# Two layer seams, the first transfers and the rings of the second mixer's queries in a two-layer fp32 encoder

## The chip, the cores and the metric

The kernel runs on one core of a Trainium2 chip. The metric is the device time of one execution in microseconds; of several runs the median counts. PE is TensorE (matmuls), DVE is VectorE, ACT is ScalarE, POOL is GpSimd; SP only issues DMAs. Each engine works through its own list of instructions in order and waits on semaphores for the others.

## The reference, cut to what matters

The input `x` is (1, 1024, 1024): 1024 tokens of width 1024; `mem` holds 256 memory tokens. There are two layers. Each normalises `x`, projects it once, runs a token mixer and beside it four cross-attention heads into the memory, brings both through one output projection, normalises that, adds the residual, and ends with a gated feed-forward block (ConvGLU, width 2816, depthwise convolution of width 3 along the tokens).

- Layer 0's mixer is a windowed grouped-query attention with rotary positions and sinks.
- Layer 1's mixer (HGRN2) has 8 heads of width 128. It is a gated linear recurrence over the tokens, forwards and backwards: a query q with a SiLU, two forget gates f and b, a value v, an output gate gs; each head's output is normalised over its 128 values and multiplied by a gain.

All of it is float32.

## The kernel before

**Products.** An fp32 operand is held as a high part (rounded, `...h`) and a low part (the rest, `...l`); a product of two such operands is three matmuls (`mm3`). A weight piece of 128 x 1024 floats (512 KB) is loaded into one of four staging buffers (`st`, pool `stage`), cast by ACT to its high part (`wh`), and DVE subtracts to get the low part (`wl`); `wunit` does this, into a ring of four. The staging buffer is free when DVE has subtracted.

**Order of the work.** A tile framework turns the program into one list per engine, by program order, priorities (`tc.high_priority(AHEAD)`) and placement hints (`tc.issue_after(x)`: not ahead of x), and sets the semaphores. A tile from a pool with `bufs=n` waits until the readers of the tile it replaces are done. So every edit can shift the order elsewhere.

**Stages in order.** (1) The start: memory tokens `mT`, the gains `gT` and the first weights are loaded (`start`, L1335 on); ACT makes `mh = mT * gT`, and PE computes the memory's keys and values of both layers, stored to DRAM (`kvd`). (2) The projections and attention of layer 0, to about 420 us. (3) Its output projection and feed-forward block. (4) The second mixer (`hgrn`), about 1235 to 1915 us. Each head projects q, f, b, v, gs (`proj_fm`, `proj_tm`); q is made in two halves of 512 tokens (b = 0, 1), each read by two of the head's four directions, taken in the order (forward, half 0), (backward, half 1), (forward, half 1), (backward, half 0). POOL writes `qin = EP * q` (L1209) as the last reader of q in a direction. `cross_head` loads one memory head's keys and values (`kvh`, `kvl`). `output` normalises the head's result (`on`), PE transposes it (`pt`, L1259), and for the last head ACT and DVE make from it high and low parts of the projection's operand (`uh`, `ul`). (5) The output projection of layer 1 (`Out.finish`): two column halves, 8 token blocks each; for the second half, of each block of 128 tokens: the matmuls into `pb`, sum of squares, `x` = residual plus normalised result, stored to `h1d`, then `norm_T`: `nu` = normalised `x`, 8 PE transposes into `pt`, and a split into `uh`, `ul`. (6) The second feed-forward block (`ffn`): `plain` computes its first unit directly (gi, gj with `wg`, ui, uj with `wu`: `X`, `Y`, `V` banks); the further units use operands that are sums and differences of `uh`/`ul` (`operands`, among them `u7l`) with the weights loaded at L662 and L666.

## Time and profile before

| | |
|---|---|
| three runs | 2661.21, 2664.71, 2666.81 us |
| median | 2664.71 us |
| the profiled execution's own time | 2661.84 us |
| its span, first to last instruction | 2659.7 us |
| PE busy | 2601.1 us (98%) |
| DVE, ACT, POOL busy | 1818.5, 1378.5, 469.6 us |
| DMA | 425.93 MB, 160 GB/s on average |

PE is the engine that is nearly always busy, so what it waits for is what there is to gain or lose. In a row of the timeline stand: start, duration, engine, line, operation, output <- inputs, and in brackets the idle time before it and what ended it. In a row of waits: engine and tile, what it waited for, total us, times, longest. In a row of windows: the stretch, its length, busy time and instructions of PE, of its weight loads, DVE, ACT and POOL, the granted PE clock, the DMA engines' share and GB/s. A queue on SP or ACT (`SPq`) is one on which DMAs are issued.

### The profile page before, as it was taken

Reading aid. Unit: us, or ns where it says so; the run is one execution under the profiler, and the core shown is the slowest. Engines: PE = TensorE matmul, PEld = TensorE weight load, DVE = VectorE, ACT = ScalarE, POOL = GpSimd, SP = SyncE. Lnnn points to the kernel's source line nnn. Section 1 sums busy time; section 2 is a strip of 40 time slices with the busy share of each in tenths; the row PEclk is TensorE's granted clock in tenths of the full one; section 3 lists DMA queues with packets and bytes.
Section 4 is the critical chain, followed back from the end, with each engine's and each line's share of the span. In section 5 each row is a group of like instructions: output and inputs, shape, how many; then the busy total and the mean of one; then the engine's idle time right before and its main releaser. Section 6 shows DMA issues by size and latency. Waiting matters only on the chain.

```text
span 2659.7 us, 39101 instructions
## 1 busy us (share of the span) xinstructions
PE 2601.1 (98%) x14420; PEld 2184.7 (82%) x14420; DVE 1818.5 (68%) x3043; ACT 1378.5 (52%) x2503; POOL 469.6 (18%) x519
## 2 busy tenths in 40 slices
PE   8999999999999999999999999999999999999998
PEld 7888887788888888887888878888888788888887
DVE  6778886578655565478688686887757755656447
ACT  6467676545444445455464554555534444445443
POOL 0321010211111100031224131231211111110013
PEclk9999999999999999999999999999999999999999
DMA  9782232367777857674236351103436778775666
GB/s 354 247 172 57 74 90 82 103 190 193 199 202 193 210 153 257 191 249 150 84 112 153 82 124 52 52 25 103 134 124 178 193 193 209 198 203 166 225 191 237
DMA packets 195728, 425.93 MB, mean 160 GB/s; under 512 B 20048, under 2 KB 56272, under 8 KB 189904
## 3 DMA queue, kind: packets, MB, share of 16 engines
q1 hardware_dynamic: 161840, 325.11, 37.9%
q0 software_dynamic: 24544, 90.19, 16.4%
q10 hardware_dynamic: 9152, 8.14, 1.0%
q8 instruction: 113, 1.85, 0.3%
q14 instruction: 79, 0.65, 0.1%
HBM read 330.04 MB, written 116.39 MB: 168 GB/s over the span
## 4 chain that ended last, share of the span: by engine, by line
PE 82%; DVE 10%; ACT 3%; DMA 3%; issue 1%; POOL 1%; SPq 0%; ACTq 0%; DVEq 0%; POOLq 0%
PE X L557 29%; PE V L557 11%; PE pj L81 6%; PE pj L82 6%; PE pj L83 6%; PE Y L557 5%; PE pb L81 4%; PE pb L83 4%; PE pb L82 4%; DVE E L1146 1%; PE po L1249 1%; PE pt L383 1%; DVE ER L1181 1%; PE pt L116 1%; PE pu L1225 1%
## 5 line engine op out<-in xcount | busy, mean ns | idle before, releaser
L87 DVE TENSOR_TENSOR wl<-st,wh 128x1024 fp32r<-128x1024 f32 (+1 forms) x238 | 262.3, 1109 | 318.8 <-ACT wh L86 280.1
L86 ACT CAST wh<-st 128x1024 fp32r<-128x1024 f32 (+1 forms) x238 | 222.4, 937 | 287.6 <-PE X L557 190.3
L81 PE MATMUL pj<-uh,wh 128*128 128x512 f32 x512 | 202.9, 397 | 4.8 <-DVE q L1091 2.6
L557 PE MATMUL X<-wl,wh 128*128 128x512 f32 x528 | 204.7, 390 | 0.0
L557 PE MATMUL X<-wh,wl 128*128 128x512 f32 x528 | 204.6, 389 | 0.0
L82 PE MATMUL pj<-ul,wh 128*128 128x512 f32 x512 | 201.7, 394 | 0.1
L83 PE MATMUL pj<-uh,wl 128*128 128x512 f32 x512 | 201.7, 394 | 0.0
L557 PE MATMUL X<-wh 128*128 128x512 f32 x528 | 198.7, 390 | 0.9 <-ACT c L963 0.9
L81 PE MATMUL pj<-wh,uh 128*128 128x384 f32 (+1 forms) x512 | 189.7, 371 | 4.7 <-DVE gs L1077 2.5
L83 PE MATMUL pj<-wh,ul 128*128 128x384 f32 (+1 forms) x512 | 187.2, 366 | 0.0
L82 PE MATMUL pj<-wl,uh 128*128 128x384 f32 (+1 forms) x512 | 186.7, 365 | 0.0
L77 DVE TENSOR_TENSOR wl<-st,wh 128x1024 fp32r<-128x1024 f32 (+1 forms) x92 | 116.7, 1275 | 26.4 <-ACT wh L76 25.7
L557 PE MATMUL V<-uh,wh 128*128 128x512 f32 x344 | 133.8, 389 | 0.0
L557 PE MATMUL V<-ul,wh 128*128 128x512 f32 x344 | 133.8, 389 | 0.0
L557 PE MATMUL V<-uh,wl 128*128 128x512 f32 x344 | 133.8, 389 | 0.0
L76 ACT CAST wh<-st 128x1024 fp32r<-128x1024 f32 (+1 forms) x98 | 98.8, 1014 | 47.8 <-PE pj L82 25.4
L557 PEld LDWEIGHTS X<-wh 128*128 128x128 f32 x528 | 99.1, 188 | 21.9 <-ACT c L963 1.3
L81 PEld LDWEIGHTS pj<-uh,wh 128*128 128x128 f32 x512 | 96.3, 188 | 24.9 <-DVE q L1091 3.5
L557 PEld LDWEIGHTS X<-wl,wh 128*128 128x128 f32 x528 | 99.1, 188 | 20.7 <-DVE wl L87 0.3
L557 PEld LDWEIGHTS X<-wh,wl 128*128 128x128 f32 x528 | 99.1, 188 | 20.6
L932 POOL TENSOR_TENSOR c<-c,g 128x512 f32<-128x512 f32 x24 | 43.7, 1838 | 388.5 <-PE X L557 160.1
L83 PEld LDWEIGHTS pj<-uh,wl 128*128 128x128 f32 x512 | 96.2, 188 | 18.7
(399 smaller groups left out, 7212.6 us busy)
## 6 DMA issues: line engine op xcount, KB each, us to landing
st<-hid SPq DMA_DIRECT2D x154, 256.0 KB, 3.0
st<-in_ffw_dram SPq DMA_DIRECT2D x108, 256.0 KB, 3.1
w2s<-in_ffw_dram POOLq DMA_DIRECT2D x24, 1024.0 KB, 9.0
st<-in_ffw_dram SPq DMA_DIRECT2D x46, 512.0 KB, 4.4
hid<-tt SPq DMA_DIRECT2D x88, 256.0 KB, 4.8
st<-w2s SPq DMA_DIRECT2D x88, 256.0 KB, 3.4
sx<-in_ffw_dram SPq DMA_DIRECT2D x84, 256.0 KB, 3.9
sy<-in_ffw_dram SPq DMA_DIRECT2D x42, 512.0 KB, 6.9
```

Source lines behind the costliest of these rows:

```text
L76: act.copy(h[:, :n], raw)
L77: (eng or dve).tensor_tensor(l[:, :n], raw, h[:, :n].bitcast(F32), op=ALU.subtract)
L81: pe.matmul(o, ah, bh, start=first, stop=False)
L82: pe.matmul(o, ah, bl, start=False, stop=False)
L83: pe.matmul(o, al, bh, start=False, stop=last)
L86: act.copy(h, src)
L87: dve.tensor_tensor(l, src, h.bitcast(F32), op=ALU.subtract)
L116: pe.transpose(ps[:, k, :], u[:, (4 * b + k) * P:(4 * b + k + 1) * P], ident)
L383: pe.transpose(tp[:, j, :], sm[:, j, c * P:(c + 1) * P], ident)
L557: last = pe.matmul(o, x, y, start=new, stop=e, skip_group_check=not first)
L932: pool.tensor_tensor(y[q][:, t, :], y[q][:, t, :], g3[:, c], op=ALU.mult)
L1146: dve.tensor_tensor_scan(B[:, rev], smask, a_[:, rev], 0.0, op0=ALU.mult, op1=ALU.add)
```

## The change

- **Start.** The first 128 rows of `mT` are issued first on SP, the next on ACT; the first weight piece comes in three parts of 256, 256 and 512 columns, not in two halves.
- **Second mixer.** q is taken from two rings, one for each half of the tokens: two buffers for half 0 and one for half 1, not one ring of three. The load of keys and values in layer 1 gets priority.
- **Seam 1.** The last transposes of the mixer (last head, half 0) are put behind the matmuls of the projection's third token block; their tiles are moved to the projection's pool, and the gain is copied by POOL. The first weights of the second feed-forward block (`wg`) are loaded early, into tiles that share the space of `qin`.
- **Seam 2.** The last two token blocks keep `nu` in a staging buffer each; their transposes stand behind the 24 matmuls of gi.
- In `operands`, the sum `more` gets the priority that its split has.

```diff
-    def norm_T(pl, pst, src, g, dh, dl, t, tag="n"):
+    def norm_T(pl, pst, src, g, dh, dl, t, tag="n", kept=None):
...
+        u = pl.tile([P, D], F32, tag=tag + "u", name=tag + "u") if kept is None else kept
...
+        def turn():
+            for b in range(2):
...
+        if kept is None:
+            turn()
+        return turn
...
-        nc.sync.dma_start(raw, kvd[l][h])
+        with tc.high_priority(AHEAD) if l else nullcontext():
+            nc.sync.dma_start(raw, kvd[l][h])
...
-                self.cross(ps, t, True, False)
+                crossed = self.cross(ps, t, True, False)
...
+                if l == 1 and i == 2:
+                    with tc.issue_after(crossed.ins):
+                        self.last(psp.tile([P, 4, P], F32, tag="pt", name="pt"))
...
-            self.first = wunit(A["ffw1"][l, 0, :, :1024], pl=self.wf) if l == 0 else None
+            self.first = wunit(A["ffw1"][l, 0, :, :1024], pl=self.wf, tags=(None, ("qin0", "qin1"))[l])
...
-                norm_T(wp, psp, x, g2, uh, ul, t)
-            psp.release()
+                kept = stg.tile([P, D], F32, tag="st", name="nu") if l and t in self.order[6:] else None
+                turn = norm_T(wp, psp, x, g2, uh, ul, t, kept=kept)
+                if kept is not None:
+                    self.turns.append(turn)
...
-            some(wg, gi, range(KT), ti, True)
+            done = some(wg, gi, range(KT), ti, True)
+            for turn in wo.turns:
+                with tc.issue_after(done.ins):
+                    turn()
...
-                more(q, x, B[1], kk, ALU.subtract)
                 with tc.high_priority(AHEAD):
+                    more(q, x, B[1], kk, ALU.subtract)
                     out_of(split, 7, kk, q)
...
+        wo1.wf = tc.alloc_tile_pool(name="hgi", bufs=1, side="right", reuse_waits="tile")
...
-                    q = eq.tile([P, 512], F32, tag="q", bufs=3, name="q")
+                    q = eq.tile([P, 512], F32, tag=f"q{b}", bufs=2 - b, name="q")
...
+            final = h == 7 and b == 0
+            on = (wo1.w1 if final else wp).tile([P, 4, P], F32, tag="on", bufs=1, name="on")
...
+                if final:
+                    pool.tensor_copy(gain, bng[:, h:h + 1])
+                    wo1.last = last
+                else:
+                    last(bank("pt"))
...
-            qin = [wp.tile([P, T], F32, tag=f"qin{d}", bufs=1, name="qin") for d in range(2)]
+            qin = [wo1.wf.tile([P, T], F32, tag=f"qin{d}", bufs=1, name="qin") for d in range(2)]
...
-        for k in (0, 2):
-            act.dma_start(mT[:, k:k + 2], A["memT"][:, k:k + 2])
+        nc.sync.dma_start(mT[:, 0:1], A["memT"][:, 0:1])
+        act.dma_start(mT[:, 1:2], A["memT"][:, 1:2])
+        act.dma_start(mT[:, 2:4], A["memT"][:, 2:4])
...
-        for p in range(2):
-            nc.sync.dma_start(raw0[:, p * 512:(p + 1) * 512], A["wmk"][0, 0, :, p * 512:(p + 1) * 512])
+        for c in (slice(0, 256), slice(256, 512), slice(512, 1024)):
+            nc.sync.dma_start(raw0[:, c], A["wmk"][0, 0, :, c])
```

**Seam 1 on PE.** Before: the last matmuls of the first two token blocks (`pb_18460`, `pb_18487`), the transposes of `on` into `pt`, and the first matmuls of the third block (`pb_18514`).

```order
L83 MATMUL pb_18460<-xwh_18178,ul_78 128x512
L83 MATMUL pb_18487<-xwh_18178,ul_78 128x512
L1259 MATMUL pt_18251<-ident_74,on_18246 128x128 x4
L81 MATMUL pb_18514<-wh_17982,oh_18515 128x512
L82 MATMUL pb_18514<-wl_17983,oh_18515 128x512
L83 MATMUL pb_18514<-wh_17982,ol_18516 128x512
```

After: the third block's last matmuls, the same transposes, and the fourth block (`pb_18548`).

```order
L82 MATMUL pb_18514<-xwl_18184,uh_77 128x512
L83 MATMUL pb_18514<-xwh_18183,ul_78 128x512
L1284 MATMUL pt_18538<-ident_74,on_18251 128x128 x4
L81 MATMUL pb_18548<-wh_17987,oh_18549 128x512
L82 MATMUL pb_18548<-wl_17988,oh_18549 128x512
```

The four transposes moved behind all 18 matmuls of the third block.

**Seam 2 on PE.** Before: the end of the last token block (`pb_19277`), the transposes of the block before it, then gi (`X_19396`).

```order
L83 MATMUL pb_19277<-xwh_18708,ol_19302 128x512
L116 MATMUL pt_19263<-ident_74,nu_19256 128x128 x4
L116 MATMUL pt_19270<-ident_74,nu_19256 128x128 x4
L557 MATMUL X_19396<-uh_77,wh_19384 128x512
L557 MATMUL X_19396<-ul_78,wh_19384 128x512
```

After: the end of gi (`X_19374`, its weights in the space of `qin`), the transposes of both last blocks (`nu_19268`, `nu_19333`), two matmuls of ui (`Y_19375`, weights `wu`), two on the first weight loaded at L686 (`X_19569`), and ui again.

```order
L576 MATMUL X_19374<-uh_77,qin1_18728 128x512
L118 MATMUL pt_19402<-ident_74,nu_19268 128x128 x4
L118 MATMUL pt_19409<-ident_74,nu_19268 128x128 x4
L118 MATMUL pt_19416<-ident_74,nu_19333 128x128 x4
L118 MATMUL pt_19423<-ident_74,nu_19333 128x128 x4
L576 MATMUL Y_19375<-uh_77,wh_19368 128x512
L576 MATMUL Y_19375<-ul_78,wh_19368 128x512
L576 MATMUL X_19569<-uh_77,wh_19527 128x512
L576 MATMUL X_19569<-ul_78,wh_19527 128x512
L576 MATMUL Y_19375<-uh_77,wl_19369 128x512
```

gi moved ahead of the transposes of the last block but one, and the last block's transposes, which stood behind gi, ui and one further matmul, moved ahead of ui.

**Seam 2 on SP.** Before: `wu` (`st_19392`) and the first two pieces of L662 and L666 stand among the reads of the cross heads' results (`ol`), ahead of the first store of `h1d`.

```order
L465 DMA ol_18987<-oT1_58 128x4x128
L75 DMA st_19392<-in_ffw1_dram 128x1024
L662 DMA st_19496<-in_ffw1_dram 128x1024
L666 DMA st_19497<-in_ffw1_dram 128x512
L465 DMA ol_19066<-oT1_58 128x4x128
L542 DMA h1d1_60<-x_18680 128x1024
```

After: `wu` (`st_19370`) and the first piece (`st_19503`) stand behind the stores of the last two blocks.

```order
L503 DMA x_19318<-h2d_61 128x1024
L555 DMA h1d1_60<-x_19253 128x1024
L555 DMA h1d1_60<-x_19318 128x1024
L75 DMA st_19370<-in_ffw1_dram 128x1024
L686 DMA st_19503<-in_ffw1_dram 128x1024
L586 DMA cw_19355<-in_conv_w_dram 128x66
```

Both loads moved behind all eight stores of `h1d`.

More of the change, by code (lines that the diff above doesn't have):

```diff
@@ L82, in mm3 @@
         pe.matmul(o, ah, bl, start=False, stop=False)
-        pe.matmul(o, al, bh, start=False, stop=last)
+        return pe.matmul(o, al, bh, start=False, stop=last)
     def split(h, l, src):
@@ L469, in cross @@
                 c = slice((k % 2) * 512, (k % 2 + 1) * 512)
-                mm3(ps, oh[:, i, :], ol[:, i, :], wh[:, c], wl[:, c], first and i == 0, last and i == 3)
+                done = mm3(ps, oh[:, i, :], ol[:, i, :], wh[:, c], wl[:, c], first and i == 0, last and i == 3)
+            return done
         def begin(self, psb, tags, y0, behind={}):
@@ L597, in plain @@
         def plain(f):
-            wg = wo.first if wo.first else wunit(A["ffw1"][l, f, :, :1024])
+            wg = wo.first
             wu = wunit(A["ffw1"][l, f, :, 1024:])
@@ L884, in ffn @@
         u2p.release()
-        if wo.wf:
-            wo.wf.release()
+        wo.wf.release()
         yp = tc.alloc_tile_pool(name=f"fy{l}", bufs=1, reuse_waits="tile")
@@ L1256, in output, with turned, last @@
                                          op0=ALU.mult, op1=ALU.mult)
-            tp = bank("pt")
-            for c in range(4):
-                pe.transpose(tp[:, c, :], on[:, c, :], ident)
-            if h == 7:
-                tp = tp.rearrange("p c t -> p (c t)")
-                oh, ol = (x[:, 7, b * 512:(b + 1) * 512] for x in (uh, ul))
-                act.activation(oh, tp, AF.Identity, scale=bng[:, h:h + 1])
-                dve.scalar_tensor_tensor(ol, tp, bng[:, h:h + 1], oh.bitcast(F32), op0=ALU.mult, op1=ALU.subtract)
+            def turned(tp):
+                for c in range(4):
+                    pe.transpose(tp[:, c, :], on[:, c, :], ident)
+                return tp.rearrange("p c t -> p (c t)")
+            def last(tp):
+                tp = turned(tp)
+                oh, ol = (x[:, 7, b * 512:(b + 1) * 512] for x in (uh, ul))
+                act.activation(oh, tp, AF.Identity, scale=gain[:, 0:1])
+                dve.scalar_tensor_tensor(ol, tp, gain[:, 0:1], oh.bitcast(F32), op0=ALU.mult, op1=ALU.subtract)
+            if h == 7:
+                gain = wo1.w1.tile([P, 1], F32, tag="gain", bufs=1, name="gain") if final else bng[:, h:h + 1]
+                if final:
+                    pool.tensor_copy(gain, bng[:, h:h + 1])
+                    wo1.last = last
+                else:
+                    last(bank("pt"))
                 return
+            tp = turned(bank("pt")).rearrange("p (c t) -> p c t", t=P)
             ot = wp.tile([P, 512], F32, tag="ot", bufs=1, name="ot").rearrange("p (c t) -> p c t", c=4)
```

34 lines of the change are left out of this document (19 added, 15 removed).

## The prediction

> **What bounds the kernel now.** I read the page's head first, then the waits of PE (TensorE), then the table by windows, then the timeline at each place that the change touches.
>
> ```profile
> span 2659.7 us, 39101 instructions
> PE 2601.1 (98%) x14420; PEld 2184.7 (82%) x14420; DVE 1818.5 (68%) x3043; ACT 1378.5 (52%) x2503; POOL 469.6 (18%) x519
> PE ps L357 <- DVE mx L360: 8.9, 14, 1.5
> PE pb L81 <- ACT mh L1351: 7.6, 1, 7.6
> PE pj L81 <- DVE q L1091: 2.6, 2, 1.6
> PE pt L1259 <- DVE on L1255: 2.3, 1, 2.3
> PE X L557 <- DVE u7l L87: 1.9, 2, 1.7
> PE pt L116 <- DVE nu L112: 1.4, 1, 1.4
> PE Y L557 <- DVE wl L87: 0.5, 1, 0.5
> ```
>
> PE is busy 2601.1 of 2659.7 us. Only its 58.6 us of idle time, and the time in which it runs at half clock, can change, because no matmul goes away. The waits say where the idle time is (total, count, longest): 8.9 us in the attention, 7.6 at the start, 2.6 for the second mixer's q, 2.3 at its end (`on`), and 1.4 + 1.9 + 0.5 around the seam into the second feed-forward layer. The diff aims at all of these but the first.
>
> **The start.** PE's 7.61 us end with `mh`, for which ACT waits on memory's transposed tokens; afterwards the weights arrive at the pace of the DMA engines.
>
> ```profile
> 7.05 0.91 ACT L1351 ACTIVATE mh<-mT,gT 128x256 fp32r<-128x256 f32 x2 [3.04 <-DMA mT<-in_memT_dram]
> 0.00:20.00 20.00, 12.33 (x83) 11.88 (x84) 10.03 (x19) 12.89 (x24) 1.16 (x7) 1.00 0.91 341
> 16.51 1.05 ACT L76 CAST wh<-st 128x1024 fp32r<-128x1024 f32 x1 [1.07 <-DMA st<-in_wmk_dram]
> 17.60 1.22 DVE L77 TENSOR_TENSOR wl<-st,wh 128x1024 fp32r<-128x1024 f32 x1 [0.58 <-ACT wh L76]
> 19.19 0.37 PE L81 MATMUL pb<-mh,wh 128*128 128x256 f32 x1
> ```
>
> The first 128 rows now come alone, ahead of the rest, so ACT need not wait 3.04 us for 256 KB; I allow 2.7 of it. But the fourth weight unit is cast at 16.51 only because its DMA has just landed (ACT waited 1.07 for it), its low part is ready at 17.60 + 1.22 = 18.82, and PE starts on it at 19.19 (the third matmul, 0.3 later, is the first to read the low part). Over these 20 us the DMA engines are 91% busy, and the bytes ahead of this unit are the same. So PE can come there at most about 18.82 − 0.3 = 18.5: a gain of 0.7, whatever it gains before. I take −0.6, with −2.7 (nothing binds) and +0.5 (two more DMA issues on SP, and smaller pieces) as ends.
>
> **The second mixer's q and its memory keys.** Two waits on q make 2.6 us:
>
> ```profile
> 1551.03 0.60 ACT L1053 ACTIVATE q<-pj 128x512 f32<-128x512 f32 x1 [3.46 <-POOL qin L1209]
> 1553.80 0.50 PE L81 MATMUL pj<-uh,wh 128*128 128x512 f32 x1 [1.57 <-DVE q L1091]
> ```
>
> ACT cannot write the new q until POOL has read the old one (`qin`, L1209). With one ring of three buffers I expected the new second half to take the buffer of the old first half, which is read last. In the compiled program it is not so: already before, it waits for the third of the four directions, which reads the old second half, and with two rings it waits for the same instruction. From the first head to 1900 us the order on PE, ACT, DVE and POOL, and what each waits for of the others, are the same in both but for a few waits at the two ends. Term: 0; ends −2.6 (both waits gone) and 0. The loads of keys and values keep their place on SP in three heads of four; the first moves ahead of three small loads, and would hold them if it waited. If that cover is gone, PE stands for their first reader, at most some 2 us by the stand of 1.57 above. Term: 0.
>
> **Seam 1, from the second mixer to its output projection.**
>
> ```profile
> 1913.53 0.28 ACT L100 ACTIVATE junk<-po 128x128 bf16<-128x128 f32 x1 [1.37 <-PE po L1249]
> 1914.19 0.63 PE L83 MATMUL pb<-xwh,ul 128*128 128x512 f32 x2
> 1915.54 1.01 POOL L93 TENSOR_TENSOR ors<-oms,nhalf 128x4 f32<-128x4 f32 x1 [7.25 <-DVE oms L91]
> 1916.58 1.12 DVE L1255 SCALAR_TENSOR_TENSOR on<-po,ors,gs 128x128 f32<-128x128 f32 x4 [0.60 <-POOL ors L93]
> 1917.08 1.16 PE L1259 MATMUL pt<-ident,on 128*128 128x128 f32 x4 [2.25 <-DVE on L1255]
> 1917.89 0.77 PE L81 MATMUL pb<-wh,oh 128*128 128x512 f32 x1
> 1920.59 0.42 PE L81 MATMUL pb<-xwh,oh 128*128 128x512 f32 x1
> 1921.09 0.39 PE L83 MATMUL pb<-xwh,ol 128*128 128x512 f32 x1
> 1921.32 0.39 PE L81 MATMUL pb<-xwh,oh 128*128 128x512 f32 x1
> ```
>
> PE stands 2.25 us for `on`, and pays again after it: six matmuls take 2.70 us (1917.89 to 1920.59) where six at the later pace (0.23 from 1921.09 to 1921.32) take 1.36, and the four transposes 0.81 where 0.4 is usual. PE ran at half clock there: 1.7 us more. The change puts 18 matmuls of another token between: 18 × 0.227 = 4.1 us, from 1914.85 to 1918.95. But the preload of the feed-forward's first weights now stands ahead of this chain on ACT and DVE, since its target is free at the last `po`: a cast of 1.05 on ACT ahead of the squares (1913.3 to 1914.35, so these end at 1915.95 and not 1915.1), a subtraction of 1.22 on DVE (to 1915.6) and two sums of 0.68 (to 1916.95) ahead of `oms`. Then POOL's 1.0 with its hand-overs: `on` starts near 1918.3, and PE, which followed its start by 0.5 (1916.58, 1917.08), could transpose at 1918.8, just when the 18 are done; the last column may cost 0.25. Term: −2.25 + 0.25 − 1.7 = −3.7; ends −4.0, and −1.7 if the chain comes a microsecond later and half the clock's price stays.
>
> The Trainium skill ("TensorE: Matmul & The Clock Gate", Part 1) puts half clock after an idle window of about 3.4 us; here a stand of 2.25 us sufficed, so the measurement decides. By the skill's rule seam 1 would bring 2.0 and seam 2 cost nothing in clock (rival D).
>
> **Seam 2, from the output projection to the second feed-forward layer.**
>
> ```profile
> 1996.58 0.60 ACT L100 ACTIVATE junk<-pb 128x512 bf16<-128x512 f32 x1 [2.71 <-PE pb L83]
> 1999.64 0.75 DVE L541 SCALAR_TENSOR_TENSOR x<-y,prs,x 128x512 f32<-128x512 f32 x1
> 2002.68 1.27 DVE L112 SCALAR_TENSOR_TENSOR nu<-x,nrs,g 128x1024 f32<-128x1024 f32 x1
> 2009.36 2.35 DVE L77 TENSOR_TENSOR wl<-st,wh 128x1024 fp32r<-128x1024 f32 x2
> 2011.27 1.04 ACT L86 CAST wh<-st 128x1024 fp32r<-128x1024 f32 x1
> 2012.89 1.22 DVE L87 TENSOR_TENSOR wl<-st,wh 128x1024 fp32r<-128x1024 f32 x1
> 2014.22 0.39 PE L83 MATMUL pb<-xwh,ol 128*128 128x512 f32 x1
> 2015.97 1.06 PE L116 MATMUL pt<-ident,nu 128*128 128x128 f32 x8 [1.37 <-DVE nu L112]
> 2028.03 1.04 PE L116 MATMUL pt<-ident,nu 128*128 128x128 f32 x8
> 2071.86 0.50 PE L557 MATMUL X<-u7l,wh 128*128 128x512 f32 x1 [1.66 <-DVE u7l L87]
> st<-in_ffw_dram SPq DMA_DIRECT2D x2, 512.0 KB, 4.3
> x<-h2d SPq DMA_DIRECT2D x1, 512.0 KB, 3.2
> ```
>
> Before, PE waits 1.37 us for the last token but one, then has 49 matmuls ahead of the last token's transposes. After, 24 matmuls (5.45 us, from 2014.45 to 2019.9) stand ahead of the transposes of both tokens. The last token's chain, by an undisturbed copy: squares at 1996.58, `x` done at 2000.39 (3.8 later), `nu` done at 2003.95 (7.4 later, with one low part of 0.7 in front). So after: squares at 2014.65, `x` at 2018.5, `nu` at 2021.4 to 2022. PE has transposed the other token by 2020.7 and waits; all transposes are done by 2022.8 to 2023.6.
>
> Now the weights. `nu` of both tokens lies in two of the four staging buffers, and on SP the loads of `wu` and the first `a1` now stand behind the last store of `h1d`, which waits for `x`. So `wu` is issued at 2018.9 and `a1` at 2019.3; the landing takes 3.2 to 4.3, and each cast 1.04 on ACT, one after the other: `wu` ready at 2023.2 to 2024.3, `a1` at 2024.2 to 2025.4. PE's order asks for two matmuls on `wu`, two on `a1`, then the rest. Idle between 2019.9 and then: at most 2025.4 − 2019.9 − 1.6 (transposes) − 0.9 (four matmuls) = 3.0, at least 1.9. Against 1.37: +1.6. Behind it lies the wait of 1.66 for `u7l`, at the end of a dense stretch of DVE. DVE's stretch starts 4.4 us earlier (transposes at 2023.6, not 2028.0) but takes over four subtractions that stood before it (2.35 for two, 1.22, and one more like it: 4.8), so `u7l` stays within half a microsecond, and PE, 1.6 later, waits hardly at all. Without the clock: 0. With a half-clock window as in seam 1: +1.7. Two stands of 1 to 1.5 us with work between lie between 2.25 (clock lost) and 1.57 (kept, at 1553.80), so I take half, +0.8. Ends: −3.5 (1.37, 1.66 and the 0.5 for `wl` all go, and no new wait) and +5 (3.0 and 1.7, and `u7l` late by another 2).
>
> **The rest.** A priority raised for `more`, and the ranks that shift with the new instructions, reorder PE between 162 and 227 us and 630 and 690 us.
>
> ```profile
> 162.00:227.00 65.00, 62.69 (x369) 56.50 (x368) 50.10 (x135) 44.24 (x116) 13.86 (x17) 1.00 0.60 133
> 630.00:690.00 60.00, 59.40 (x262) 48.75 (x262) 38.92 (x42) 30.49 (x39) 7.03 (x8) 1.00 0.77 207
> ```
>
> PE is idle there for 2.3 and 0.6 us: term 0, ends ±2.5.
>
> **Sum.** −0.6 + 0 − 3.7 + 0.8 + 0 = −3.5 us. The profiled execution took 2661.84 us (2659.7 of span and 2.1 around it), so 2658.3; it lies 2.9 below the median of the runs, 2664.71, so I forecast a median of 2661.2.
>
> **Rivals.** *A: the q rings do open.* Both waits of 1.57 and 1.04 go: −2.6 more, 2658.6. For it: the rings are the change's own subject, and PE's gaps are there. Against it: the same instruction is waited for. 0.13.
> *B: seam 2 comes out clean.* `wu` lands in 3.2 or less, no clock is lost, and DVE's stretch ends early, so 1.37 + 1.66 + 0.5 go: −0.6 − 3.7 − 3.5 = −7.8, 2656.9. Against it: `nu` of the last token is not there before 2021.4. 0.18.
> *C: the staging ring binds (slower).* With two of four buffers held by `nu`, loads go in pairs: landing 4.3, cast 1.04, subtraction 1.22, so 6.6 us a pair. If PE needs the pair after `wu` and `a1` within that time, it waits 6.6 once more, with 3.0 + 1.7 − 1.37 before: −0.6 − 3.7 + 3.3 + 6.6 = +5.6, 2670.3. It decides once the third load is asked for less than 6.6 us after the first two; PE's order has some 80 matmuls (18 us) before that, which speaks against it. 0.1.
> *D: half clock does not hang on stands as short as these.* Then the slow window at 1917 stays wherever PE stands, and seam 2 adds none: −0.6 − 2.0 + 0 = −2.6, 2662.1. Against it: the slow matmuls begin with the stand's end. 0.06. This is what the skill's rule would make of it.
> The forecast itself: 0.53.
>
> **Numbers.** 0.2% of 2664.71 is 5.3 us, about what a measurement of this kernel can tell from no change. Faster by more: B (0.18), A (0.13, −6.1), and 0.04 of the forecast's tail: 0.35. Slower by more: C, 0.1; nothing else reaches it. The rest, 0.55, is within. The range holds A and B and the forecast's own ends (seam 2 late by 3 and the reordered stretches by 2.5): 2654.5 to 2667.
>
> **What would show it.** First matmul near 5 us but PE's weights late near 18 us; the q waits at L1077 and L1115 still 1.6 and 1.0; no stand before `on`'s transposes, and eighteen matmuls ahead of them at full clock; PE waiting for `nu` and then for `wu` between gi and Y, about 3 us in all. Wrong: q's waits gone, PE idle at 0 in seam 2, or more than 5 us idle in the attention's reordered part.

## The result and the profile after

The changed kernel takes 2667.82 us (median of 21 runs, 2663.07 to 2673.45), the kernel before 2663.61 us on the same chips (21 runs, 2659.74 to 2667.73). The ratio is 1.0014, with a 95% interval of 1.0008 to 1.0020: slower by about 3.7 us, still inside 0.2%. The forecast was 2661.2 us, 3.5 us faster than before, with a range up to 2667.0. So the sign of the sum was wrong and the median lies 0.8 us outside the range. The profiled execution took 2666.74 us.

The head of the page after, and PE's waits (us in total, count, longest):

```profile
span 2664.8 us, 39117 instructions
PE 2607.9 (98%) x14420; PEld 2187.6 (82%) x14420; DVE 1819.9 (68%) x3043; ACT 1379.7 (52%) x2503; POOL 468.4 (18%) x520
PE pb L81 <- ACT mh L1388: 5.8, 2, 5.4
PE pt L390 <- ACT sm L383: 3.0, 3, 2.2
PE pt L118 <- DVE ul L87: 3.0, 3, 1.5
PE Y L576 <- ACT wh L76: 2.0, 1, 2.0
PE pj L81 <- DVE q L1115: 2.0, 2, 1.1
PE X L576 <- DVE u7l L87: 0.3, 1, 0.3
```

The waits that the change aimed at did shrink: the start from 7.6 to 5.8, `on` from 2.3 to nothing, `u7l` from 1.9 to 0.3. In their place stand a wait for `sm` in the attention (2.2 the longest), one for `ul` and one for `wh` at the second seam. Idle time is 2664.8 − 2607.9 = 56.9 us, 1.7 less than before. But PE's busy time has grown by 6.8 us, from 2601.1 to 2607.9, with the same 14420 matmuls, which is more than the 5.1 us by which the span is longer. Some 4 of the 6.8 us are matmuls at half clock: by the clock's record PE was busy at half clock for 12.1 us instead of 6.7, which costs 2.7, and 1.3 more lie in the first 20 us. About 1 us is a slower pace behind the first seam (below). The rest is open. Four places tell it. Their windows after (the window, its length, PE, PEld, DVE, ACT and POOL busy, the clock granted, DMA share, GB/s):

```profile
0.00:20.00 20.00, 13.77 (x84) 12.51 (x84) 9.89 (x21) 12.71 (x23) 1.15 (x7) 1.00 0.90 327
162.00:227.00 65.00, 62.05 (x354) 55.68 (x354) 48.61 (x133) 43.44 (x114) 14.73 (x17) 0.97 0.56 135
1900.00:2000.00 100.00, 100.00 (x540) 82.90 (x539) 57.30 (x96) 42.88 (x92) 20.44 (x23) 1.00 0.43 140
2020.00:2040.00 20.00, 16.17 (x66) 12.27 (x65) 14.68 (x17) 7.42 (x12) 2.38 (x3) 0.83 0.95 295
```

**The start.** Rows of the timeline after:

```profile
5.41 0.58 PE L81 MATMUL pb<-mh,wh 128*128 128x256 f32 x1 [5.41 <-ACT mh L1388]
16.94 1.05 ACT L76 CAST wh<-st 128x1024 fp32r<-128x1024 f32 x1 [1.34 <-DMA st<-in_wmk_dram]
20.34 1.28 DVE L1389 SCALAR_TENSOR_TENSOR ul<-x,gT,uh 128x1024 fp32r<-128x1024 f32 x1
22.82 0.50 PE L82 MATMUL pb<-wl,mh 128*128 128x512 f32 x1 [0.27 <-DVE wl L77]
```

PE starts 2.2 us earlier, at 5.41, and after 20 us has done 84 matmuls where it had done 83: the early ones ran slowly, 13.77 us for 84 instead of 12.33 for 83, and the fourth weight unit is cast at 16.94 where it was 16.51. Then ACT and DVE come in another order: before, the first token piece `ul` began at 18.98, ahead of the memory's sums, and now it stands at 20.34 between them and the `wl` that PE needs at 22.5. Counted by the same matmul, PE is 2.2 us ahead at the first, 0.6 at the fortieth, 0.1 at the 83rd, and 0.4 behind at the 120th (27 us). The record of the clock begins only at 12.7 us, so the 1.00 of the first window says nothing of the matmuls ahead of that. They follow each other every 0.21 us (128 x 256), and every 0.12 from 13.1 us on. In all thirteen profiles the slow pace lasts until 11.6 to 14.0 us, whether PE begins at 5.2 or at 7.6, so an earlier start is worth at most about half of what it looks.

**The attention at 208 us.** Rows of the timeline, first of after, then of before:

```profile
207.25 0.86 POOL L142 DMA_DIRECT2D w2s<-w2s  x1
208.04 0.33 SPq L193 DMA_DIRECT2D kvl<-kvd  x1
215.74 0.62 ACT L195 CAST kvh<-kvl 128x512 fp32r<-128x512 f32 x1 [5.41 <-DMA kvl<-kvd]
216.93 1.99 PE L390 MATMUL pt<-ident,sm 128*128 128x128 f32 x8 [2.23 <-ACT sm L383]
```

```profile
208.44 0.88 POOL L136 DMA_DIRECT2D w2s<-w2s  x1
208.96 0.33 SPq L186 DMA_DIRECT2D kvl<-kvd  x1
213.01 0.62 ACT L188 CAST kvh<-kvl 128x512 fp32r<-128x512 f32 x1 [1.83 <-DMA kvl<-kvd]
```

The keys and values of the next head (`kvl`, 256 KB) landed 4.0 us after their issue before, and 7.7 us now: as soon as they are there, ACT, which has waited for them, casts them (208.96 to 213.01; 208.04 to 215.74). ACT's cast of them stands in its queue ahead of the scaling of `sm`, so PE waits 2.23 us and pays again with slow transposes: eight in 1.99 us. From the matmul before to one shortly behind, PE goes from 1.8 us ahead of before to 2.1 behind. That is 3.9 us. Over the whole reordered stretch, 160 to 230 us, it loses 2.3.

**Seam 1.** Rows of the timeline after:

```profile
1913.05 1.13 DVE L1280 SCALAR_TENSOR_TENSOR on<-po,ors,gs 128x128 f32<-128x128 f32 x4 [0.28 <-POOL ors L93]
1915.27 0.60 PE L1284 MATMUL pt<-ident,on 128*128 128x128 f32 x4
```

`on` is ready (1914.2) before the eighteen matmuls in front of its transposes end, PE does not stand, and the clock stays full: PE is busy for all of the 100 us from 1900. Counted by the same matmul it wins 3.9 us from 1908 to 1924. Then it gives 1.0 back by 2012 without any stand: the matmuls that read `oh` and `ol` follow each other 5 to 8 ns later than before. All eight profiles with this seam show this loss (1.0 to 1.1 us) and none of the others; its cause is open.

**Seam 2.** Rows of the timeline after:

```profile
2020.52 0.32 SPq L555 DMA_DIRECT2D h1d<-x  x1
2020.89 1.13 SPq L75 DMA_DIRECT2D st<-in_ffw_dram  x1
2022.07 0.44 SPq L686 DMA_DIRECT2D st<-in_ffw_dram  x1
2024.53 1.25 PE L118 MATMUL pt<-ident,nu 128*128 128x128 f32 x8 [1.45 <-DVE ul L87]
2026.70 1.04 ACT L76 CAST wh<-st 128x1024 fp32r<-128x1024 f32 x1 [2.84 <-DMA st<-in_ffw_dram]
2027.80 0.79 PE L576 MATMUL Y<-uh,wh 128*128 128x512 f32 x1 [2.02 <-ACT wh L76]
2029.38 0.80 PE L576 MATMUL X<-uh,wh 128*128 128x512 f32 x1 [0.36 <-ACT wh L86]
2033.38 0.42 PE L576 MATMUL Y<-uh,wh 128*128 128x512 f32 x1
```

The order is the one that the prediction named: `x` of the last block, its store, then `wu` and `a1`. `wu` is issued at 2020.89 and its cast begins at 2026.70, so it took 5.8 us to land; `a1` took 6.2. PE stands 1.45 + 2.02 + 0.36 = 3.83 us, and the clock granted from 2020 to 2040 is 0.83: the matmuls take 0.43 us each until 2033, eleven of them 5.2 us where 2.5 is usual.

### The profile page after: what moved, and what is told of

The parts are those of the page before. It is cut to its first block, busy times and chain, and to the rows that moved or that the text cites. A ratio compares the mean times of both kernels' runs of the same rounds, so it can differ in the third digit from the quotient of the medians.

```text
span 2664.8 us, 39117 instructions
## 1 busy us (share of the span) xinstructions
PE 2607.9 (98%) x14420; PEld 2187.6 (82%) x14420; DVE 1819.9 (68%) x3043; ACT 1379.7 (52%) x2503; POOL 468.4 (18%) x520
## 3 DMA queue, kind: packets, MB, share of 16 engines
q0 software_dynamic: 24544, 90.19, 16.2%
## 4 chain that ended last, share of the span: by engine, by line
PE 82%; DVE 11%; DMA 3%; ACT 3%; issue 1%; POOL 1%; SPq 0%; ACTq 0%; DVEq 0%; POOLq 0%
PE X L576 28%; PE V L576 11%; PE pj L81 6%; PE pj L82 6%; PE pj L83 6%; PE Y L576 5%; PE pb L83 4%; PE pb L82 4%; PE pb L81 4%; DVE E L1170 1%; PE po L1273 1%; PE pt L390 1%; DVE ER L1205 1%; DVE wl L77 1%; PE pu L1249 1%
## 5 line engine op out<-in xcount | busy, mean ns | idle before, releaser
L82 PEld LDWEIGHTS pj<-ul,wh 128*128 128x128 f32 x512 | 96.3, 188 | 18.6 <-DVE ul L87 0.4
```

Source lines behind the costliest of these rows:

```text
L82: pe.matmul(o, ah, bl, start=False, stop=False)
```

## The experiments

Eleven kernels ran, in three groups, each with its own runs of before on the same chip. "Alone" is the kernel before with one part of the change; "all but" is the changed kernel with parts undone.

| kernel | parts of the change in it | median us (runs) | ratio to before (95%) |
|---|---|---|---|
| the change | all | 2667.82 (21) | 1.0014 (1.0008–1.0020) |
| start_alone | start | 2667.59 (11) | 1.0008 (0.9999–1.0017) |
| seam1_alone | seam 1 | 2662.31 (11) | 0.9994 (0.9985–1.0002) |
| after_seam2_undone | all but seam 2 | 2662.52 (11) | 1.0000 (0.9991–1.0009) |
| seam2_weights_early | all but start; weights moved | 2665.24 (11) | 1.0005 (0.9996–1.0014) |
| all_but_start | all but start | 2662.85 (11) | 1.0000 (0.9991–1.0008) |
| all_but_start_and_seam2 | seam 1, rings, precedence | 2658.87 (11) | 0.9985 (0.9976–0.9994) |
| start_copy_later | start; one copy moved | 2661.60 (11) | 0.9996 (0.9988–1.0005) |
| start_memory_only | half of the start | 2661.18 (11) | 0.9996 (0.9987–1.0005) |
| rings_keys_precedence | rings, precedence | 2665.32 (11) | 0.9999 (0.9988–1.0011) |
| first_seam_copy_later | all but seam 2; copy moved | 2657.70 (7) | 0.9976 (0.9964–0.9987) |
| first_seam_memory_pieces | all but seam 2 and half of the start | 2656.92 (11) | 0.9974 (0.9965–0.9982) |

0.0010 is 2.7 us. The intervals are about ±2.4 us wide, and the difference of two rows is uncertain by about ±3.4 (±2.9 against the row of the whole change), so a part's price rests on several rows that agree, and on the traces. The medians of before in the three groups are 2663.27, 2663.55 and 2664.26 us (33, 33 and 23 runs). The ratio is not the quotient of the medians; the text goes by the ratio and says so where it goes by medians.

**The start alone.**

```diff
-            act.dma_start(mT[:, k:k + 2], A["memT"][:, k:k + 2])     # k = 0, 2
+        nc.sync.dma_start(mT[:, 0:1], A["memT"][:, 0:1])
+        act.dma_start(mT[:, 1:2], A["memT"][:, 1:2])
+        act.dma_start(mT[:, 2:4], A["memT"][:, 2:4])
-            nc.sync.dma_start(raw0[:, p * 512:(p + 1) * 512], A["wmk"][0, 0, :, p * 512:(p + 1) * 512])
+        for c in (slice(0, 256), slice(256, 512), slice(512, 1024)):
+            nc.sync.dma_start(raw0[:, c], A["wmk"][0, 0, :, c])
```

> The kernel before with the new order of the first transfers alone. Theory (the start costs): first matmul near 5.4 us and not 7.6, half clock until about 12.9 all the same, every weight from the second unit on landing 0.4 us later, PE 0.8 later at 65 us; and since this edit alone also reorders the attention's lists, the memory keys' load meets the DRAM-to-DRAM sums again: ACT waits some 5 us for it near 215 and PE 2.2. In all +1.5 to +3.5 us against the kernel before. Rival (those are chance differences between two profiled executions): within 1 us of the kernel before, no such wait of PE near 215.

Measured 1.0008: +2.1 us, with an interval that just takes in 0 (+4.3 by the medians). The timeline has the same stand in the attention as the whole change, with the load issued 0.78 us behind the copy:

```profile
217.63 0.62 ACT L195 CAST kvh<-kvl 128x512 fp32r<-128x512 f32 x1 [5.60 <-DMA kvl<-kvd]
218.81 2.05 PE L390 MATMUL pt<-ident,sm 128*128 128x128 f32 x8 [2.42 <-ACT sm L383]
```

So neither the rings nor the seams bring it in. The reordering itself comes from here too: PE's order from 162 to 226 us differs from before in the five kernels with the whole start in them, and in no other kernel.

**Seam 1 alone.**

```diff
+                if l == 1 and i == 2:
+                    with tc.issue_after(crossed.ins):
+                        self.last(psp.tile([P, 4, P], F32, tag="pt", name="pt"))
+            self.first = wunit(A["ffw1"][l, 0, :, :1024], pl=self.wf, tags=(None, ("qin0", "qin1"))[l])
+            final = h == 7 and b == 0
```

> The kernel before with seam 1 alone: the last transposes behind the third token block's matmuls, the first feed-forward weights preloaded into the space of qin. Theory: the wait of 2.25 for the normalised output is gone and no half-clock stretch follows, so -3.5 to -4.0 us. Rival (the half-clock stretch belongs to its place and not to the wait, or the preload delays the chain): -2.0 or less.

Measured 0.9994, −1.6 us with an interval from −4.0 to +0.5: too wide to settle 3.7. The number lies on the rival's side, but the trace shows neither a stand nor a slow stretch at the seam. It shows the seam itself as forecast (by the same matmul 5.0 us behind before ahead of the seam, 1.1 behind it: −3.9). Those 5.0 us come from other places, most of them from slow stretches near 120 and 157 us and from a stand of 1.82 us with one near 1034. And it shows something not forecast, the wait for `u7l` 160 us later:

```profile
PE X L576 <- DVE u7l L87: 0.5, 2, 0.3
```

Before it was 1.9 in total with 1.7 the longest. So the first seam's part brings this, not the second's; that it is the early load of `wg`, whose subtraction leaves DVE's stretch behind the seam, is argued and was not tried apart. It is worth 1.5 us (2068 to 2072). With 1.3 us that the slower pace takes back in between, seam and `u7l` together are −4.1 us.

**Seam 2 undone in the changed kernel.**

```diff
-                kept = stg.tile([P, D], F32, tag="st", name="nu") if l and t in self.order[6:] else None
+                kept = None
-            if l:
-                self.pst = psp
-            else:
-                psp.release()
+            psp.release()
```

> The changed kernel with seam 2 undone: the last two token blocks are transposed where they were before, nothing is kept in the staging buffers. Theory (seam 2 costs what its two stands and its slow stretch show, less what it took away): 3 to 4.5 us faster than the changed kernel, so about 0 against the kernel before. Rival (seam 2 is neutral, and the loss lies in the start and the attention): as slow as the changed kernel, +4.

Measured 1.0000 against 1.0014 for the whole change: the second seam costs 3.7 us (±2.9).

**The weights of the second seam asked for early** (all but the start; `wu` and `a1` take their staging buffers, and are loaded, ahead of the two kept rows).

```diff
+                if l and t == self.order[6]:
+                    self.wu = wunit(A["ffw1"][l, 0, :, 1024:])
+                    self.a1 = stg.tile([P, 1024], F32, tag="st", name="st")
+                    nc.sync.dma_start(self.a1, A["ffw1"][l, 1, :, 1024:])
                 kept = stg.tile([P, D], F32, tag="st", name="nu") if l and t in self.order[6:] else None
```

> The changed kernel without its start, and with the loads of wu and of the first a1 taken out of the staging ring ahead of the two kept rows, so that both are asked for before the first store of h1d. Theory (the ring's order holds the weights back): no wait for wu or a1 behind gi, at most a stand of 1.4 for the rows, no slow stretch; with seam 1 in it, -4 to -6 us against the kernel before. Rival (the last block's own chain, ready some 7 us after its last matmul, sets the end): PE stands there 2.5 us or more as in the changed kernel, so -1 to +1.

Measured 1.0005, neither the theory's −4 to −6 us nor the rival's stand; the same kernel without the edit, all_but_start below, has 1.0000. The stands at the seam are gone, and the time did not fall with them. Windows of this kernel, and rows of its timeline:

```profile
2010.00:2020.00 10.00, 10.00 (x49) 8.20 (x48) 6.05 (x12) 2.83 (x7) 1.62 (x3) 1.00 0.19 70
2030.00:2040.00 10.00, 10.00 (x45) 8.14 (x44) 3.06 (x4) 1.05 (x1) 1.72 (x2) 1.00 0.96 249
2060.00:2080.00 20.00, 15.77 (x60) 11.70 (x59) 17.50 (x18) 8.90 (x13) 3.50 (x4) 0.91 0.66 144
```

```profile
2038.36 1.05 ACT L86 CAST wh<-sx 128x1024 fp32r<-128x1024 f32 x1 [8.77 <-DMA sx<-in_ffw_dram]
2039.44 1.23 DVE L87 TENSOR_TENSOR wl<-sx,wh 128x1024 fp32r<-128x1024 f32 x1 [6.94 <-ACT wh L86]
2072.66 0.73 PE L580 MATMUL X<-u7h,wh 128*128 128x512 f32 x2 [1.95 <-ACT u7h L86]
2075.05 0.79 PE L580 MATMUL X<-u7l,wh 128*128 128x512 f32 x1 [1.66 <-DVE u7l L87]
```

PE is 100% busy from 2010 to 2040. But the loads behind now queue up in turn: the DMA engines are 19% busy from 2010 to 2020 and 96% from 2030 to 2040, a summed weight (`sx`) lands so late that ACT waits 8.77 us and DVE, in whose queue its subtraction stands ahead of other work, 6.94. This debt of DVE comes due at `u7h` and `u7l` 33 us later, with half clock (0.91); that it is this debt is argued from the order of the rows. So late weights were the stand at the seam, as theory had it, but taking that away uncovers the next limit. By the same matmul this kernel loses 5.3 us against before from 2012 to 2100, where all_but_start loses 2.0. The gain of the reordering is not there even with the weights in time.

**All but the start**, and **all but the start and seam 2.**

```diff
# both: first transfers as before
-        nc.sync.dma_start(mT[:, 0:1], A["memT"][:, 0:1])
-        act.dma_start(mT[:, 1:2], A["memT"][:, 1:2])
-        act.dma_start(mT[:, 2:4], A["memT"][:, 2:4])
+        for k in (0, 2):
+            act.dma_start(mT[:, k:k + 2], A["memT"][:, k:k + 2])
-        for c in (slice(0, 256), slice(256, 512), slice(512, 1024)):
+        for c in (slice(0, 512), slice(512, 1024)):
# the second: seam 2 undone too, as above
+                kept = None
```

> The changed kernel with the first transfers as before (rings, keys and values with precedence, both seams stay). Theory (the start costs: +0.8 us by 65 us, and some 2.3 us for the head's keys that land late behind the copy of the summed weights at 208 us, against 2.2 us won at the first matmul; it costs 2.1 us alone): 1.5 to 2.5 us faster than the whole change, so +1.5 to +2.5 us against before, and ScalarE's stand of 5.4 us for kvl near 216 us gone. Rival (the start alone read high by chance, and the whole change lost its time at the seams only): still +3.5 to +4.5 us against before.

> The changed kernel with the first transfers and the second seam as before: the rings, the keys and values with precedence and the first seam's new order are left. Theory (the start costs 2, the second seam 4 and the first seam saves 3.7 less what the later phase gives back): -1.6 to -3.7 us against before, the best of all tried here. Rival (the first seam's gain is given back behind it, since alone it showed only -1.6 with an interval that takes in 0): -0.8 to +0.5 us.

Measured 1.0000 and 0.9985: −0.7 and −4.7 us by the medians. The first is 3.7 us under the whole change (ratios 1.0014 and 1.0000), more than the start alone had shown and more than expected (+1.5 to +2.5 against before), and the 5.4 us stand of ACT is gone: its cast waits 1.9 for `kvl` and PE does not wait for `sm` there. The second gives seam 2 a second price, 4.0 us, and what is left, the first seam, −4.0 by the ratio and −4.7 by the medians, which agrees with −4.1 by the trace. By the same count seam 2 costs 4.3 us in the change and 3.1 in all_but_start: from 2012 to 2100 us they lose 3.2 and 2.0 against before, where the profiles with seam 1 and without seam 2 win 1.1 to 1.2.

**The start alone with one copy moved.** POOL's 1 MB copy of the summed weights that is asked for at 209 us in the kernel start_alone goes out one step later, with the last of them.

```diff
-        for r, a, f, n, x, add in steps:
-            ins = yield
+        for j, (r, a, f, n, x, add) in enumerate(steps):
+            if l or j < 17:
+                ins = yield
+            if l == 0 and j == 16:
+                ins = yield
```

> Before with the new first transfers alone, and GpSimd's 1 MB copy of the summed weights that is asked for at 209 us asked for one step later, at 222 us, together with the last of them; no other instruction moves on any engine that computes. Theory (the copy delays the keys and values of the next head from 4.0 to 7.8 us, and TensorE stands 2.4 us for it): kvl lands in about 4 us, ScalarE's stand of 5.6 us becomes 1.5 to 2.5, the 2.4 us stand of TensorE at 218.8 us falls under 1, and the time is 1.5 to 2.5 us under the start alone: -0.5 to +0.6 us against before. Rival (the start loses its time in the first 65 us and by the new order in the attention): the landing is shorter but the time stays at +1.5 to +2.5.

```profile
209.96 0.33 SPq L196 DMA_DIRECT2D kvl<-kvd  x1
212.62 0.62 ACT L198 CAST kvh<-kvl 128x512 fp32r<-128x512 f32 x1 [0.38 <-DMA kvl<-kvd]
```

With the copy out of the way (it goes out at 218.18 us, with the last) the same load lands in 2.6 us, PE has no stand there, and the time is 0.9996 against 1.0008 for start_alone: 3.2 us, just about the ±3.4 of such a difference. That is more than the stand of 2.42, by about the slow transposes behind it (eight in 2.05 us instead of 1.04). By the names of their tiles, PE, ACT, SP and DVE run the same instructions in the same order in both traces; on POOL the copy alone changes place. The same edit stands between after_seam2_undone (1.0000) and first_seam_copy_later (0.9976) below, 6.4 us apart, again with PE's order the same. And by the same matmul the three profiles with the collision lose 2.2 to 2.3 us against before from 160 to 230 us, while the two with the copy moved win 1.6. So the collision is shown, at 3.9 us by the traces. Without it the new order would even have been a gain: PE is busy for 66.58 of the 68 us from 162 to 230 instead of 64.95, because stands of 0.9 for `xl` and 0.8 for `rq` are gone.

**The memory's pieces alone**: before with `mT` in three pieces, but the first weight in two halves.

```diff
-        for c in (slice(0, 256), slice(256, 512), slice(512, 1024)):
+        for c in (slice(0, 512), slice(512, 1024)):
             nc.sync.dma_start(raw0[:, c], A["wmk"][0, 0, :, c])
```

> Before with the memory's first pieces as in the change (one column on SP's queue, then one and two), but the first weight in two halves as before. Theory (the first matmul comes early because of the small first weight piece, and the second unit lands late because of the same pieces): the first matmul back to 7.1 to 7.6 us, the second weight unit's landing back near 10.1 us, kvl's 5 us stand gone since the attention keeps its order there, and the time -0.5 to +0.5 us against before. Rival (the memory's pieces are what delays the transfers behind): first matmul near 6 and the second unit still 0.4 us late, +0.4 to +1 us.

```profile
5.44 0.58 PE L81 MATMUL pb<-mh,wh 128*128 128x256 f32 x1 [5.44 <-ACT mh L1389]
22.68 0.50 PE L82 MATMUL pb<-wl,mh 128*128 128x512 f32 x1 [0.77 <-DVE wl L77]
211.29 0.33 SPq L193 DMA_DIRECT2D kvl<-kvd  x1
215.36 0.62 ACT L195 CAST kvh<-kvl 128x512 fp32r<-128x512 f32 x1 [1.85 <-DMA kvl<-kvd]
```

The theory missed the start itself. The first matmul comes at 5.44 as in the whole change, so not the smaller first weight piece brings it forward but the memory's first column. And no smaller piece delays the later units: the fourth is cast at 16.3 to 17.1 us in the six profiles with the old first transfers, at 16.3 to 16.9 in the five with the new ones, at 16.2 in the two with half of them. What is common to all seven with the new or half of the new is a stand for `wl` near 23 us (0.77 here, 0.27 in the change), which the six do not have. As theory had it, the attention keeps its order, `kvl` lands in 4.0, and the time is 0.9996. So it is the split of the first weight into three pieces that brings the reordering of the attention and the collision. But the early first matmul is not what this kernel wins by: by the same matmul it is 2.4 us behind before at 300 us. It wins 2.6 us from 425 to 500, where PE's order differs from before in the two kernels with the memory's pieces alone, and PE stands for 1.14 us from 470 to 500 instead of 2.59.

**Rings, keys and precedence alone.**

```diff
-                    q = eq.tile([P, 512], F32, tag="q", bufs=3, name="q")
+                    q = eq.tile([P, 512], F32, tag=f"q{b}", bufs=2 - b, name="q")
-        nc.sync.dma_start(raw, kvd[l][h])
+        with tc.high_priority(AHEAD) if l else nullcontext():
+            nc.sync.dma_start(raw, kvd[l][h])
```

> Before with the second mixer's queries in two rings, the memory's keys and values asked for with precedence, and the precedence of the subtraction: neither the first transfers nor a seam is changed. Theory (the rings move no instruction and no wait, the precedence moves a few rows at the second mixer's first head that nobody waits for): -0.5 to +0.5 us against before, with the waits for q near 1.6 and 1.0 us as in before. Rival (part of what the first seam's kernels gained came from the rings or the precedence): -1.5 to -3 us.

```profile
PE pj L81 <- DVE q L1117: 2.7, 3, 1.2
```

Measured 0.9999. The waits for q are 2.7 us in total as before (2.6), and PE's order is the same. They do nothing here.

**Two versions without the second seam.** The first is the changed kernel with seam 2 undone and the copy moved; the second has seam 2 undone and the first weight in two halves.

```diff
# both
+                kept = None
# the first
+            if l == 0 and j == 16:
+                ins = yield
# the second
+        for c in (slice(0, 512), slice(512, 1024)):
```

> The changed kernel with the second seam as before and GpSimd's 1 MB copy of the summed weights at 208 us asked for one step later. The parts measured so far: the start with the copy moved -1.9 us against before, the first seam with rings and precedence -4.7. Theory (the parts add, and the collision of copy and keys is what the start cost): -4.5 to -6.5 us against before, the fastest here or level with the kernel that has the old first transfers. Rival (the start's early matmul is given back by its late second weight unit also without the collision): -2.5 to -4.5 us.

> The changed kernel with the second seam as before and the first weight in two halves as before; the memory's three pieces stay. Theory (these pieces alone were worth -2.4 us and the first seam -4.7, and the attention keeps its order at 208 us, so no collision): -5 to -7 us against before. Rival (both read low by chance; nothing adds): -3.5 to -5 us.

Measured 0.9976 (0.9964–0.9987) and 0.9974 (0.9965–0.9982): −6.4 and −6.9 us, faster than before by 0.24 and 0.26%, and faster than the change by over 10 us at the medians. The parts add, within the noise: −4.0 for the first seam without start and seam 2, and −1.1 for either start that does not collide (0.9996 each alone) make −5.1, and the difference from the measured is inside ±3.4. The profiled spans end 1.4 and 1.7 us earlier (2655.6 and 2655.3 against 2657.0). The same count tells where this comes from. The first wins 2.9 us over all_but_start_and_seam2 from 160 to 230 us (−1.6 against +1.3), the second 2.6 from 425 to 500. Each gives some 1.6 back to a slow stretch, near 120 and 337 us, that the profile of all_but_start_and_seam2 does not have. So both gains lie in the order of later stretches, which nobody had planned.

## Why the prediction failed

The forecast of −3.5 us met +3.7 (ratio 1.0014). By terms, 7.2 us:

- **The start, −0.6 (ends −2.7 and +0.5): measured +3.7** and +4.0 from the two pairs of kernels with and without it (1.0014 and 1.0000; 1.0000 and 0.9985), and +2.1 alone; by the trace of the change 0.8 by 65 us and 2.3 from 160 to 230. What binds the first 20 us was right: the fourth unit lands when it did, and PE's lead at the 83rd matmul is 0.3 us on the mean of five profiles against six. The step that failed is that the working ended there. It holds the order behind it for unchanged. First, the subtraction for `wl` slips behind `ul`, and the stand for it near 23 us turns 0.3 ahead into 0.4 behind at the 120th matmul (it starts at 27.0 and 26.5 us on the mean). Then, far larger, the start reorders the attention at 162 to 227 us, where the load of `kvl` comes to stand behind POOL's copy. I had put that reordering down to the raised priority of `more` and to the new instructions; all_but_start has both, and neither the new order nor the stand.
- **The rest, 0 ± 2.5: this is where that collision lay.** I read PE's idle time there as 2.3 us and let a reordering cost at most about that. The idle time after is 65 − 62.05 = 2.95, so by idle time alone nothing happened. The price was the clock and the place of the stand. The row of this window after shows 354 matmuls instead of 369 in the same 65 us, at a clock of 0.97 instead of 1.00. What could have been seen: ACT already waited for that load in before, and its order on POOL and SP was close. A reordered stretch has to be searched for transfers that come to lie 0.3 us differently, not bounded by its present idle time.
- **Seam 2, +0.8 (ends −3.5 and +5): measured +3.7 and +4.0.** The mechanism was right, down to the order of the stands; three sizes were off. The landing was taken as 3.2 to 4.3 us from rows of single loads, and was 5.8 and 6.2 (4.9 and 6.0 in all_but_start): the 512 KB store of `h1d` is issued 0.37 us ahead of `wu` and moves at the same time (that this store is the reason is argued, not tried). So the stands are 3.83 and not 3.0. The clock's price, counted half of 1.7, came whole in all_but_start (eight matmuls in 3.5 us instead of 1.8) and was 2.7 in the change. And 1.66 us for `u7l` was credited to this seam, though all but 0.3 of it belongs to the first: `u7l` waits 0.3 in seam1_alone too. With the stands and the clock as measured, and with the 0.3 left of `u7l` and the 0.5 for `wl` that do go, the same working gives 3.83 − 1.37 + 2.7 − 0.8 = 4.4, by the trace 4.3.
- **Seam 1, −3.7 (ends −4.0 and −1.7): right at the seam,** −3.9 by the trace of the change. That the total stays near it is partly luck: −1.5 at `u7l` and +1.3 from the slower pace were both not foreseen and nearly cancel. And 1.7 of the forecast was the price of a slow stretch that is not in every execution: of the five profiles with the 2.25 us stand for `on`, start_memory_only has none. It wins 1.3 us on before there, so that much and not 1.7 was the clock's; the four transposes take 0.77 us from stand to next matmul at full clock too.
- **The rings and the memory keys, 0: right,** 0.9999. Rival A falls: the waits for q stayed.

Of the rivals, B (seam 2 clean) falls. C named the right side and the staging ring as cause, but not the mechanism: no second pair of loads made PE wait 6.6 us; the first pair came late because it was issued late and landed slowly. D falls: half clock followed the stands of 1.45 and 2.02 at 2030. It followed the stand for `on` in four of the five profiles that have it, and came there in none of the eight without it. The Trainium skill ("TensorE: Matmul & The Clock Gate", Part 1) asks for an idle window of about 3.4 us; behind the first 20 us no slow stretch has a single stand longer than 2.42 us (start_alone) ahead of it, so the traces do not bear the rule out if it is read as one unbroken gap. Forecast and rivals alike had no case in which the start costs more than half a microsecond, and this is what the range lacked.

## What to carry to other kernels

An edit of the first transfers is not over when they have landed: where a scheduler sets the order, look at every engine's order in the whole program, and wherever it differs follow the DMA issues of all queues, since a shift of 0.3 us between a big background copy and a small load that an in-order engine waits for can cost more than the edit brings. Deferring work behind weights that are already there helps only if the next weights can still be asked for; rows kept in the staging ring take its buffers, and the loads wait for the last row. Price a stand on TensorE with the slow matmuls behind it, and measure the parts of a bundled change apart: here two parts were worth −6.9 us and two others gave back over 10.

## What the hardware showed that was not expected

**A load overtaken by a third of a microsecond.** The copy occupies POOL for 0.86 to 0.88 us. Where the 256 KB load was issued 0.50 to 0.52 us after the copy's start it landed in 3.5 to 4.9 us (eight profiles, before among them); at 0.78 and 0.79 us in 7.7 to 7.9 (the three with the collision), 0.2 us after the copy itself; with no copy in 2.6 or 2.7 (two). The packets of the two queues tell why. Here q0 carries the copy and q1 the load (packets, MB, share). First the change, from the load's issue to 211 us and from there to its landing; then before, for the first 2.2 us behind the load's issue, with no packet of the copy among them:

```profile
q0 software_dynamic: 48, 0.39, 78.7%
```

```profile
q0 software_dynamic: 96, 0.66, 73.4%
q1 hardware_dynamic: 144, 0.26, 17.6%
```

```profile
q1 hardware_dynamic: 65, 0.13, 53.7%
```

In before the load's packets start 0.96 us after its issue and the copy's only 2.3 us after it, so the load goes first. In the change the copy's packets start 0.78 us after the load's issue, and the load's only 2.98 us after it, then beside the copy until both are done. The Trainium skill ("DMA: Bandwidth & Descriptors", Queues, rings and completion order) says that each DMA engine takes turns between queues packet by packet. The 4.4 us in which both move here agree with that: 144 packets of the load, most of 2 KB, pass among 96 of the copy, most of 8 KB. Why the load's first packet comes 2 us late once the copy is ahead, no run here shows.

**Half clock after many short stands, and not every time.** Between 409 and 421 us PE has stands of 0.3, 0.1, 0.6, 0.2 and 0.8 us in every profile. In the profile of the change the six matmuls that follow run at half clock, in that of before they do not; of the kernels above, five profiles show it there and eight do not. Rows of after, then of before:

```profile
418.42 0.45 PE L364 MATMUL ps<-kh,qs 128*128 128x384 f32 x1 [0.83 <-DVE mx L367]
420.61 0.63 PE L83 MATMUL pb<-wh,ul 128*128 128x512 f32 x1
```

```profile
417.92 0.40 PE L83 MATMUL pb<-wh,ul 128*128 128x512 f32 x1
```

Longer stands do not settle it either. In start_memory_only PE keeps full clock behind the same stand of 2.25 us for `on` that is followed by a slow stretch in before, and in seam2_weights_early behind 2.97 us, the longest stand of all behind the first 20 us:

```profile
1917.13 1.01 PE L1286 MATMUL pt<-ident,on 128*128 128x128 f32 x4 [2.25 <-DVE on L1282]
1917.90 0.48 PE L81 MATMUL pb<-wh,oh 128*128 128x512 f32 x1
```

```profile
1868.47 0.66 PE L1252 MATMUL pt<-ident,ER 128*128 128x128 f32 x4 [2.97 <-ACT ot L1311]
```

By the clock's records a slow stretch between the start and the end lasts 3.41 us, or twice that, in each of the twelve profiles that have any, so it costs at most 1.7 or 3.4 us; the six matmuls here cost about 6 × 0.2 = 1.2. Which stretches fall into an execution differs from one to the next, and this is part of why single runs of one kernel spread over 8 us. Of the 89 runs of before beside the experiments, the eleven with a mean granted clock of 0.999 have a median of 2661.6 us, the eight with 0.996 one of 2668.7.
